# Contiguous filter features, modulation rows broadcast from DRAM, and a router product in column groups

## The chip, the cores and the metric

The kernel runs on one core of a Trainium2 chip. The metric is the device time of one execution in microseconds. TensorE (PE in the profile) multiplies a stationary operand, which it loads first (PEld), with a moving operand that streams past; VectorE (DVE), ScalarE (ACT) and GpSimd (POOL) work elementwise; SyncE (SP) issues most of the DMA transfers, in order.

## The reference

A two-layer diffusion backbone over 1024 tokens of width 1024, all in fp32. Layer 0 mixes tokens with a gated recurrence (RG-LRU) and with Hyena, which convolves with long filters that a small network of sine layers makes from positions. Layer 1 mixes with a Conformer convolution. Behind each mixer stands a mixture of 16 experts, in which every expert takes the 128 tokens that score highest for it. All parts are modulated by six vectors of width 1024 per layer, made from a conditioning vector c.

```python
# the modulation, per layer
sh1, sc1, g1, sh2, sc2, g2 = split(silu(c) @ w_mod[l] + b_mod[l], 6)
# Hyena's filters: n = 1024 positions, 2 orders, 2 directions, 512 channels
hid = sin(freq[0] * (z @ filt_w1 + filt_b1))
hid = sin(freq[1] * (hid @ filt_w2 + filt_b2))        # 1024 x 64
filt = (hid @ filt_w3 + filt_b3) * window
kf = rfft(two_sided(filt))
# behind each mixer
xl = xl + g1 * mixer(modulate(rmsnorm(xl, n1), sh1, sc1))
h = modulate(rmsnorm(xl, n2), sh2, sc2)
probs = softmax(h @ router[l], over tokens)
gates, idx = top_k(probs, 128)                         # per expert
xl = xl + g2 * scatter_add(idx, experts(h[idx]) * gates)
```

## The kernel before

**Stages.** In the order of the profiled span: constants, the filter network and the first modulation vectors (0 to 22 us); Hyena's filters, with the norm and transposes of x between them (22 to 158); the input projection and the RG-LRU (to 300); Hyena itself (to about 573), with the rest of the modulation between; the opening of w_out (to 603); the posts of layer 0, which are output projection, residual, norm and router, tile by tile of 128 tokens, with the sorting for the top tokens (to 737); the experts of layer 0 (743 to 1322); the conformer (to 1550); the posts of layer 1 (to about 1700) and its experts (1723 to 2300); the final norm.

**Order of work.** A tile framework puts the instructions of every engine in order and sets the semaphores. It does so by itself, except at the end of `even_mixer`, where PE, DVE and ACT follow the written order. SP's queue is in order: a transfer that waits holds up all behind it. `wr` is a ring of four buffers of 128 x 2048 through which the w_mod, w_in, kd and w_out loads and some results pass.

**Big products.** They run as three matmuls (L153 to L155, `mm3` or its like) on a high and a low part, which `split` makes with a ScalarE cast and a VectorE subtraction. For w_out these are `wide_hi` (L958, the cast oh) and `wide_lo` (L963, the subtraction ol).

**Filters.** `sin_layer` writes the hidden features to h2, 65 rows (the 65th is one, for the bias) by 1024 positions. `signal` in `filters` (L377 to L391) makes the filters of 128 channels, one order and both directions: for each residue a of the position modulo 8 a matmul (L387) with h2[:, a::8] as stationary operand, 65 x 128 with a step of 8 elements, and 128 columns of ws moving; L388 multiplies four of them by the window, to sd. There are 8 such jobs of 16 matmuls. The products with the Fourier matrix G follow (L410 q0, L414 and L415 qa, L419 and L420 qb), then a chain of small VectorE steps (L432 to L448), and the write to kd in DRAM (L449) from a `wr` buffer. `ada` work (L225) and the transposes of x (L302) are put between by the generator `other`.

**Modulation.** `ada_mm` (L225) multiplies silu(c) with w_mod, in four column groups, and `ada_end` turns the result into columns: mod (128 x 48, a column per 128 features) and gg, the norm weight times one plus the scale. In Hyena's stage `fill` does a part of this between other steps. `bcast` (L258 to L266) makes a 128 x 1024 tile with a row's value in all partitions out of eight such columns: eight fp32 matmuls (L264) of a column broadcast to 128 x 128 with the identity, and two ScalarE copies (L266). It is called four times a layer: g1b and G2b (`mix_cast`), sh2b (`even_mixer` and `mix_more`), g2b (the experts, behind the index copy `ixq`).

**Posts and router.** `post` (L1000 to L1032) makes tile t of x1; `post_t` transposes x1 (L1039) and copies it to hT (L1041); `post_r` (L1044 to L1050) multiplies hT, eight blocks of 128 x 128, stationary, with the 16 columns of R2 = router * gg for each, moving, and adds the rest on VectorE (L1050). They are called for the tile before, between the matmuls of the present one. From tile 3 on VectorE sorts (L879, L882) beside that.

**End of Hyena in layer 0.** `hy_inv` and its like end with VectorE steps L607 to L614 and L558 to L575, then products with IG (L625), zt (L633), and the split of y and z. In the written order after it stand the openings `wide_hi` and `wide_lo` of w_out, the broadcasts, and the split. The gate ge (ACT L716, DVE L717) is written to ycd (SP L718).

Of the kernel before, what the change touches and what calls it, by code (L numbers as in the profile page):

```python
# [9 lines left out]
F32 = mybir.dt.float32  # L10
# [135 lines left out]
class Builder:  # L146
# [22 lines left out]
    def consts(self):  # L169
# [5 lines left out]
        nc.gpsimd.memset(self.idn, 0.0)  # L175
        nc.gpsimd.affine_select(self.idn, self.idn, pattern=[[-1, 128]], compare_op=OP.not_equal,
                                fill=1.0, base=0, channel_multiplier=1)
        it = T.tile([128, 128], I32, name="it")
        nc.gpsimd.iota(it, pattern=[[1, 128]], base=0, channel_multiplier=0)
        self.iota = P.tile([128, 128], F32, name="iota")  # L180
# [54 lines left out]
    def ada_end(self, l, s, q):  # L235
        nc = self.nc
        r = self.wr.tile([128, 512], F32, name="w", tag="w")
        nc.scalar.copy(r, q)
        t = self.ps.tile([128, 512], F32, name="t", tag="n")
        for b in range(4):  # L240
            nc.tensor.transpose(t[:, b * 128:(b + 1) * 128], r[:, b * 128:(b + 1) * 128], self.idn)
        tv = t.rearrange("p (b j x) -> p j b x", b=4, j=4, x=32)
        nc.vector.tensor_tensor(self.mod[l][:, s * 16:(s + 1) * 16].rearrange("p (j b) -> p j b", j=4),
                                tv[:, :, :, 0], self.v(f"bm{l}", s * 16, 16).rearrange("p (j b) -> p j b", j=4),
                                op=OP.add)
        if l == 0 and s == 0:
            nc.vector.tensor_tensor(self.modc.rearrange("p (j b) -> p j b", j=4),
                                    tv[:, :, :, 1], self.v("bm0", 0, 16).rearrange("p (j b) -> p j b", j=4),
                                    op=OP.add)
            nc.vector.scalar_tensor_tensor(self.ggc, self.modc[:, 8:16], 1.0, self.v("n1g0"), op0=OP.add, op1=OP.mult)  # L250
        if s == 0:
            nc.vector.scalar_tensor_tensor(self.gg[l][0], self.mod[l][:, 8:16], 1.0, self.v(f"n1g{l}"),
                                           op0=OP.add, op1=OP.mult)
        if s == 2:
            nc.vector.scalar_tensor_tensor(self.gg[l][1], self.mod[l][:, 32:40], 1.0, self.v(f"n2g{l}"),
                                           op0=OP.add, op1=OP.mult)

    def bcast(self, dst, col):  # L258
        nc = self.nc
        for h in range(2):  # L260
            q = self.ps.tile([128, 512], F32, name="q", tag="n")
            for c in range(4):
                k = h * 4 + c
                nc.tensor.matmul(q[:, c * 128:(c + 1) * 128], col[:, k:k + 1].to_broadcast([128, 128]), self.idn,  # L264
                                 start=True, stop=True)
            nc.scalar.copy(dst[:, h * 512:(h + 1) * 512], q)  # L266

    def rstd(self, pool, ss, n=1):
        nc = self.nc
# [43 lines left out]
    def sin_layer(self, pool, q, m, fcol, bcol, dst):  # L313
        nc = self.nc
        x = pool.tile([128, 512], F32, name="sx", tag="sx", bufs=2)[:m]
        k = pool.tile([128, 512], F32, name="sk", tag="sk", bufs=2)[:m]
        nc.scalar.activation(x, q, AF.Identity, bias=bcol, scale=fcol)
        nc.vector.tensor_scalar(k, x, 1.0 / (2.0 * math.pi), MAGIC, op0=OP.mult, op1=OP.add)
        nc.vector.tensor_scalar(k, k, -MAGIC, None, op0=OP.add)
        nc.vector.scalar_tensor_tensor(x, k, -TWO_PI_HI, x, op0=OP.mult, op1=OP.add)  # L320
        nc.vector.scalar_tensor_tensor(x, k, -TWO_PI_LO, x, op0=OP.mult, op1=OP.add)
        nc.vector.tensor_scalar(x, x, PI_IN, -PI_IN, op0=OP.min, op1=OP.max)
        nc.scalar.activation(dst, x, AF.Sin, bias=0.0, scale=1.0)

    def filt_mlp(self, p, f):
# [9 lines left out]
        nc.sync.dma_start(w3, A["fw3"].rearrange("k (g c) -> k g c", g=4))  # L335
        self.G = p.tile([128, 8, 256], F32, name="G")
        self.Gn = p.tile([128, 3, 256], F32, name="Gn")
        self.h2 = h2 = p.tile([65, D], F32, name="h2")
        self.ws = ws = p.tile([65, 2, 2, 512], F32, name="ws")
        self.fbias = p.tile([1, 2, 512], F32, name="fbias")  # L340
        nc.gpsimd.memset(h2[64:65, :], 1.0)
        fq, b1, b2 = self.v("fq"), self.v("fb1"), self.v("fb2")
        fb = f.tile([128, 2], F32, name="fb")
        V.tensor_tensor(fb[:, 0:1], fq[:, 0:1], b1, op=OP.mult)
# [5 lines left out]
        for n in range(2):  # L350
            q = self.ps.tile([128, 512], F32, name="q", tag="n")
            nc.tensor.matmul(q[:64], w2[:, n], h1, start=True, stop=True)
            self.sin_layer(f, q[:64], 64, fq[:64, 1:2], fb[:64, 1:2], h2[:64, n * 512:(n + 1) * 512])
        w3v = w3.rearrange("k (o d) c -> k o d c", o=2)
        for o in range(2):
            V.tensor_tensor(ws[:, o, 0], w3v[:, o, 0], w3v[:, o, 1], op=OP.add)
# [14 lines left out]
    def filters(self, fk, other):  # L371
# [5 lines left out]
        def signal(qd, o):  # L377
# [5 lines left out]
            for i in range(2):  # L383
                for a in range(0, 8, 4):
                    q = self.ps.tile([128, 4, 128], F32, name="q", tag="n")
                    for j in range(4):
                        nc.tensor.matmul(q[:, j], h2[:, a + j:D:8], ws[:, o, i, cs], start=True, stop=True)  # L387
                    V.tensor_tensor(sd[:, i, a:a + 4], q, win[:, a:a + 4], op=OP.mult)  # L388
            V.tensor_tensor(sd[:1, 0, 0], sd[:1, 0, 0], sd[:1, 1, 0], op=OP.add)
            V.scalar_tensor_tensor(sd[:1, 0, 0], sd[:1, 0, 0], 0.5, self.fbias[:, o, cs], op0=OP.mult, op1=OP.add)  # L390
# [254 lines left out]
    def even_mixer(self, st, so):  # L645
# [7 lines left out]
        with ExitStack() as s1, ExitStack() as sl:  # L653
# [164 lines left out]
            with tc.tile_pool(name="pq0", bufs=1, reuse_waits="tile") as pq, \  # L818
# [5 lines left out]
                    self.wide_hi(po, ws[q])  # L824
                    self.wide_lo(po, ws[q], q)
                self.mix_cast(0)
                self.bcast(self.sh2b, self.mod[0][:, 24:32])
                self.wide_hi(po, ws[2])
                z = drain()
                self.split(th, tl, y)  # L830
# [85 lines left out]
    def mix_open(self, l, st, st2):  # L916
# [12 lines left out]
        self.W = [pm.tile([128, 128], F32, name=f"W{i}") for i in range(2)]  # L929
        self.S = [pm.tile([128, 128], F32, name=f"S{i}") for i in range(2)]  # L930
        self.nc.vector.memset(self.W[1][64:96], 0.0)
        self.R2 = pm.tile([128, 8, NE], F32, name="R2")
        self.cb = pm.tile([128, NE], F32, name="cb")

    def mix_cast(self, l):
        self.bcast(self.g1b, self.mod[l][:, 16:24])
        self.bcast(self.G2b, self.gg[l][1])

    def mix_more(self, l):
        if l:  # L940
            self.bcast(self.sh2b, self.mod[l][:, 24:32])
        self.nc.vector.tensor_tensor(self.R2, self.router, self.gg[l][1][:, :, None].to_broadcast([128, 8, NE]), op=OP.mult)
        q = self.ps.tile([128, 512], F32, name="q", tag="n")
        for c in range(8):
            self.nc.tensor.matmul(q[:, :NE], self.mod[l][:, 24 + c:25 + c].to_broadcast([128, 128]), self.router[:, c],
# [88 lines left out]
    def post_t(self, x, hT, b):  # L1034
        nc = self.nc
        q = self.ps.tile([128, 512], F32, name="q", tag="n")
        for j in range(4):
            c = b * 4 + j
            nc.tensor.transpose(q[:, j * 128:(j + 1) * 128], x[:, c * 128:(c + 1) * 128], self.idn)  # L1039
        h = self.pm.tile([128, 4, 128], F32, name="hT", tag="hT", bufs=3)  # L1040
        nc.scalar.copy(h, q)  # L1041
        hT.append(h)

    def post_r(self, t, hT, r):  # L1044
        nc = self.nc
        V = nc.vector
        q = self.ps.tile([128, 512], F32, name="q", tag="n")
        for c in range(8):
            nc.tensor.matmul(q[:, :NE], hT[c // 4][:, c % 4], self.R2[:, c, :], start=c == 0, stop=c == 7)  # L1049
        V.scalar_tensor_tensor(self.lg[:, t], q[:, :NE], r, self.cb, op0=OP.mult, op1=OP.add)  # L1050
        if t == 3:
            self.todo += [lambda: self.soft(0), self.group0]
# [125 lines left out]
    def experts(self, l):  # L1178
        nc, tc, A = self.nc, self.tc, self.A
        V = nc.vector  # L1180
        with tc.tile_pool(name=f"pe{l}", bufs=1, side="right", reuse_waits="tile") as pe:
# [83 lines left out]
            with tc.issue_after(getattr(self.last, "ins", self.last)):  # L1265
                for _ in range(4):
                    self.moe_load(nc.gpsimd)
            with tc.issue_after(self.ixq):
                self.bcast(g2b, self.mod[l][:, 40:48])
            fetch(1)  # L1270
            for b in range(2):
                transx(0, b)
# [264 lines left out]
    def build(self):  # L1537
        nc, tc, A = self.nc, self.tc, self.A
        with ExitStack() as st:
# [5 lines left out]
            self.kd = [[dr.tile([128, 8, 2, 128], F32, name=f"kd{o}{h}") for h in range(4)] for o in range(2)]  # L1545
            self.ycd = dr.tile([D, D], F32, name="ycd")
            self.hsd = dr.tile([512, D], F32, name="hsd")
            self.acc = [dr.tile([D, D], F32, name=f"acc{l}") for l in range(2)]
            self.h2d = [dr.tile([D, D], F32, name=f"h2d{l}") for l in range(2)]
            self.ud = [dr.tile([128, D], F32, name=f"ud{n}") for n in range(8)]  # L1550
# [78 lines left out]
```

## Time and profile before

| | |
|---|---|
| three runs | 2336.77, 2337.35, 2340.97 us; median 2337.35 |
| span of the profiled execution | 2336.7 us |
| granted TensorE clock, mean | 0.959 of full speed |
| PE / DVE / ACT busy | 94% / 78% / 52% |
| data moved | 611.9 MB, 262 GB/s |
| the costliest lines | L153 to L155 (big products), their casts (L158) and subtractions (L159) |

The profiled execution's own time is its span, 2336.7 us, some 0.7 under the median. Its critical chain follows, from the last instruction back, what released each step; its lines are the start, the duration and what ran, with x for the number of passes of a matmul. An fp32 matmul has two passes. A row of a group gives line, engine, operation, out<-in, partitions x elements, the count, then busy time, the mean of one, and the idle time before it with what ended it.

### The profile page before, as it was taken

The page shows a single profiled execution, that of the slowest core. Times are in us where ns is not written, and L with a number is a line of the kernel's source. Part 1 is how long each engine was busy: PE and PEld are TensorE (multiplying, and loading weights), DVE is VectorE, ACT ScalarE, POOL GpSimd, SP SyncE. Part 2 cuts the span into 40 slices and gives each one's busy share as a digit, 9 for nine tenths or more (in the row PEclk, how much of TensorE's full clock was granted, in tenths as well). Part 3 has the DMA queues.
Part 4 walks back from the last instruction along what each step waited for, and adds up shares of the span by engine and source line. Part 5 has one row for each costly group of instructions (what it writes and reads, how often), then busy time and mean ns, then how long its engine had stood idle before and what let it go on. Part 6 is the DMA issues. An engine that isn't in the chain of part 4 may idle for free.

```text
span 2336.7 us, 29325 instructions
## 1 busy us (share of the span) xinstructions
PE 2195.2 (94%) x10970; PEld 1734.1 (74%) x10970; DVE 1820.5 (78%) x2871; ACT 1203.8 (52%) x1454; POOL 126.8 (5%) x128
## 2 busy tenths in 40 slices
PE   7999999998995999999999699989869999999997
PEld 5987765776883787787787578878747777777775
DVE  4577888998586898898988642455968888988887
ACT  2537921123221777777777531134237676776775
POOL 0000000000001000000000100010010000000001
PEclk8889999999997999999999899989979999999999
DMA  6341277554657999999998634424579999999974
GB/s 232 108 145 45 81 299 279 198 201 184 207 184 278 338 377 393 375 383 385 379 391 302 180 120 117 136 73 180 186 290 371 374 369 386 369 378 379 367 283 153
DMA packets 208776, 611.91 MB, mean 262 GB/s; under 512 B 27828, under 2 KB 76534, under 8 KB 198841
## 3 DMA queue, kind: packets, MB, share of 16 engines
q1 hardware_dynamic: 197386, 568.62, 64.6%
q0 software_dynamic: 11248, 41.42, 7.2%
q8 instruction: 86, 1.41, 0.2%
q14 instruction: 56, 0.46, 0.1%
HBM read 554.43 MB, written 55.57 MB: 261 GB/s over the span
## 4 chain that ended last, share of the span: by engine, by line
PE 82%; DVE 9%; DMA 4%; ACT 2%; issue 1%; SPq 0%; POOL 0%; POOLq 0%; ACTq 0%; DVEq 0%
PE P L153 20%; PE P L155 20%; PE P L154 20%; PE P L1237 6%; PE q L387 3%; PE q L1202 2%; PE q L225 2%; PE q L586 1%; PE q L625 1%; PE q L1049 1%; DMA w<-i_w_mod 1%; DMA wx<-i_exp_w 1%; PE q L503 1%; PE q L1368 1%; PE q L302 1%
## 5 line engine op out<-in xcount | busy, mean ns | idle before, releaser
L159 DVE TENSOR_TENSOR e<-wx,e 128x1024 fp32r<-128x1024 f32 x516 | 618.9, 1221 | 92.4 <-ACT e L158 78.4
L158 ACT CAST e<-wx 128x1024 fp32r<-128x1024 f32 x516 | 540.9, 1053 | 231.6 <-PE P L155 231.0
L153 PE MATMUL P<-e,th 128*128 128x512 f32 x1384 | 562.5, 406 | 0.2 <-ACT th L158 0.2
L155 PE MATMUL P<-e,tl 128*128 128x512 f32 x1384 | 543.3, 393 | 1.6 <-DVE tl L159 1.6
L154 PE MATMUL P<-e,th 128*128 128x512 f32 x1384 | 542.7, 392 | 0.0
L154 PEld LDWEIGHTS P<-e,th 128*128 128x128 f32 x1384 | 260.6, 188 | 60.5 <-DVE e L159 4.3
L153 PEld LDWEIGHTS P<-e,th 128*128 128x128 f32 x1384 | 260.4, 188 | 60.6 <-issue 7.2
L155 PEld LDWEIGHTS P<-e,tl 128*128 128x128 f32 x1384 | 260.1, 188 | 60.4 <-DVE tl L159 2.5
L159 DVE TENSOR_TENSOR e<-w,e 128x1024 fp32r<-128x1024 f32 x176 | 211.8, 1222 | 50.9 <-ACT e L158 28.3
L153 PE MATMUL P<-hh,wh 128*128 128x512 f32 x576 | 229.3, 399 | 8.1 <-DVE y L762 4.2
L158 ACT CAST e<-w 128x1024 fp32r<-128x1024 f32 x176 | 183.8, 1050 | 95.1 <-PE P L155 75.6
L155 PE MATMUL P<-hh,wlo 128*128 128x512 f32 x576 | 228.7, 397 | 1.8 <-DVE wlo L159 1.8
L154 PE MATMUL P<-hl,wh 128*128 128x512 f32 x576 | 229.1, 398 | 0.7 <-DVE ms L271 0.7
L153 PEld LDWEIGHTS P<-hh,wh 128*128 128x128 f32 x576 | 109.4, 190 | 42.9 <-issue 19.3
L155 PEld LDWEIGHTS P<-hh,wlo 128*128 128x128 f32 x576 | 109.4, 190 | 28.4 <-issue 4.0
L154 PEld LDWEIGHTS P<-hl,wh 128*128 128x128 f32 x576 | 109.2, 190 | 28.2 <-issue 5.2
L1301 POOL DMA_INDIRECT acc<-yo,ix x31 | 50.7, 1634 | 933.1 <-DVE yo L1300 933.1
L159 DVE TENSOR_TENSOR tl<-q,th 128x512 fp32r<-128x512 f32 x128 | 84.6, 683 | 6.6 <-ACT th L158 4.7
L158 ACT CAST wh<-w 128x1024 fp32r<-128x1024 f32 x16 | 16.7, 1049 | 136.7 <-PE P L154 124.2
L1237 PE MATMUL P<-wx,xf 128*128 128x512 f32 x176 | 79.1, 592 | 0.0
L1041 ACT COPY hT<-q 128x512 f32<-128x512 f32 x32 | 18.6, 588 | 110.4 <-PE q L1039 110.4
L158 ACT CAST th<-q 128x512 fp32r<-128x512 f32 x128 | 71.6, 585 | 1.8 <-PE q L1202 1.8
(403 smaller groups left out, 3216.5 us busy)
## 6 DMA issues: line engine op xcount, KB each, us to landing
wx<-i_exp_w SPq DMA_DIRECT2D x272, 1024.0 KB, 7.9
w<-i_exp_w SPq DMA_DIRECT2D x96, 1024.0 KB, 7.9
w<-i_w_mod SPq DMA_DIRECT2D x48, 1024.0 KB, 8.0
wst<-i_w_in SPq DMA_DIRECT2D x20, 512.0 KB, 5.1
kd<-w SPq DMA_DIRECT2D x8, 1024.0 KB, 5.2
w<-kd SPq DMA_DIRECT2D x8, 1024.0 KB, 7.0
acc<-res SPq DMA_DIRECT2D x16, 512.0 KB, 2.9
e<-i_exp_w SPq DMA_DIRECT2D x16, 512.0 KB, 5.9
```

The costliest lines, as they stand in the source:

```text
L153: t.matmul(o, lh, rh, start=start, stop=False)
L154: t.matmul(o, lh, rl, start=False, stop=False)
L155: t.matmul(o, ll, rh, start=False, stop=stop)
L158: self.nc.scalar.copy(hi, src)
L159: self.nc.vector.tensor_sub(lo, src, hi.bitcast(F32))
L225: self.nc.tensor.matmul(self.ada_q[32 * j:32 * j + 32, :], self.sp[:, kc, :], w[:, j * 512:(j + 1) * 512], start=kc == 0, stop=kc == 7, ti ...
L302: nc.tensor.transpose(q[:, t * 128:(t + 1) * 128], x[:, c * 128:(c + 1) * 128], self.idn)
L387: nc.tensor.matmul(q[:, j], h2[:, a + j:D:8], ws[:, o, i, cs], start=True, stop=True)
L503: nc.tensor.matmul(q[:, :n], W, xa[:, o:o + n], start=True, stop=True)
L1202: nc.tensor.transpose(q[:, j], src[:, c * 128:(c + 1) * 128], self.idn)
L1237: nc.tensor.matmul(P[:, ns], f[:, k], h[:, ns], start=k == 0, stop=k == 7)
L1301: self.last = nc.gpsimd.indirect_dma_start(self.acc[l][:, :], bass.IndirectOffsetOnAxis(ap=xT[e][1][:, 0:1], axis=0), yo, None, compute_op ...
```

## The change

There are three parts. First, h2 is stored as 65 x 8 x 128, by residue, so that the stationary operand of L387 is contiguous; `sin_layer` writes it in the order of positions through a view with 128 elements between neighbours. Second, for the last four of the six vectors, `ada_end` transposes the columns to rows (two matmuls), copies them to a `wr` buffer (the r that it has already), and writes them to a DRAM tensor rowd of 4 x 1024; `bcast` is then one DMA of a row to all 128 partitions. The order that g2b had behind `ixq` is gone. Third, the router: R2, padded with zeros to 32 columns for each block, is the stationary operand, each of its eight blocks in one of four column groups of 32, with the 128 tokens of hT moving. This gives four partial sums in four groups of partitions; ScalarE copies them to L4, and one more matmul, with a 128 x 16 matrix of four stacked identities, adds and transposes them. hT has two buffers instead of three.

The core of the diff:

```diff
@@ consts
+        self.stack = P.tile([128, NE], F32, name="stack")
+        nc.vector.tensor_tensor(self.stack, self.idn[:, 0:NE], self.idn[:, 32:32 + NE], op=OP.add)
+        for g in (64, 96):
+            nc.vector.tensor_tensor(self.stack, self.stack, self.idn[:, g:g + NE], op=OP.add)
@@ ada_end, bcast
-
-    def bcast(self, dst, col):
-        nc = self.nc
-        for h in range(2):
+        cols = {1: [self.mod[l][:, 16:24], self.mod[l][:, 24:32]], 2: [self.gg[l][1], self.mod[l][:, 40:48]]}
+        if s in cols:
             q = self.ps.tile([128, 512], F32, name="q", tag="n")
-            for c in range(4):
-                k = h * 4 + c
-                nc.tensor.matmul(q[:, c * 128:(c + 1) * 128], col[:, k:k + 1].to_broadcast([128, 128]), self.idn,
-                                 start=True, stop=True)
-            nc.scalar.copy(dst[:, h * 512:(h + 1) * 512], q)
+            for i, col in enumerate(cols[s]):
+                nc.tensor.transpose(q[:8, i * 128:(i + 1) * 128], col, self.idn)
+            rows = r[:8, :256].rearrange("c (i p) -> c i p", i=2)
+            nc.scalar.copy(rows, q[:8, :256].rearrange("c (i p) -> c i p", i=2))
+            nc.sync.dma_start(self.rowd[l][2 * s - 2:2 * s].rearrange("i (c p) -> c i p", p=128), rows)
+
+    def bcast(self, dst, l, i):
+        self.nc.sync.dma_start(dst, self.rowd[l][i:i + 1, :].to_broadcast([128, D]))
@@ sin_layer, filt_mlp, signal
+        if len(dst.shape) == 3:
+            x = x.rearrange("m (p a) -> m p a", a=8)
         nc.scalar.activation(dst, x, AF.Sin, bias=0.0, scale=1.0)
...
-        self.h2 = h2 = p.tile([65, D], F32, name="h2")
+        self.h2 = h2 = p.tile([65, 8, 128], F32, name="h2")
...
-                        nc.tensor.matmul(q[:, j], h2[:, a + j:D:8], ws[:, o, i, cs], start=True, stop=True)
+                        nc.tensor.matmul(q[:, j], h2[:, a + j], ws[:, o, i, cs], start=True, stop=True)
@@ mix_open, post_t, post_r
-        self.R2 = pm.tile([128, 8, NE], F32, name="R2")
+        self.R2 = pm.tile([128, 8, 32], F32, name="R2")
+        self.nc.vector.memset(self.R2, 0.0)
...
-        h = self.pm.tile([128, 4, 128], F32, name="hT", tag="hT", bufs=3)
+        h = self.pm.tile([128, 4, 128], F32, name="hT", tag="hT", bufs=2)
...
+        q4 = self.ps.tile([128, 512], F32, name="q", tag="n")
+        for c in range(8):
+            g = 32 * (c % 4)
+            nc.tensor.matmul(q4[g:g + 32, :128], self.R2[:, c], hT[c // 4][:, c % 4], start=c < 4, stop=c > 3,
+                             tile_position=(0, g))
+        L = self.pm.tile([128, 128], F32, name="L4", tag="L4", bufs=1)
+        nc.scalar.copy(L, q4[:, :128])
         q = self.ps.tile([128, 512], F32, name="q", tag="n")
-        for c in range(8):
-            nc.tensor.matmul(q[:, :NE], hT[c // 4][:, c % 4], self.R2[:, c, :], start=c == 0, stop=c == 7)
+        nc.tensor.matmul(q[:, :NE], L, self.stack, start=True, stop=True)
@@ the experts
-            with tc.issue_after(self.ixq):
-                self.bcast(g2b, self.mod[l][:, 40:48])
+            self.bcast(g2b, l, 3)
```

The calls of `bcast` become (self.g1b, l, 0), (self.sh2b, l, 1) and (self.G2b, l, 2).

The instructions around the edits move too. First VectorE at the end of layer 0's Hyena part, where the last inverse transform ends; before (line, operation, out<-in, size), with ge the gate, ol the low part of w_out and E the result that the last products need:

```order
L717 TENSOR_TENSOR ge<-ge,hsr 128x1024
L611 TENSOR_TENSOR sub<-E,w 128x1024
L612 TENSOR_TENSOR pq<-pq,sub 128x8x128
L717 TENSOR_TENSOR ge<-ge,hsr 128x1024
L613 TENSOR_TENSOR E<-pq 128x1024
L614 TENSOR_TENSOR E<-pq 128x1024
L558 TENSOR_TENSOR sub<-E 128x512
...
L575 SCALAR_TENSOR_TENSOR pq<-sub,E 128x2x128
L963 TENSOR_TENSOR ol<-w,oh 128x2048 x2
L633 TENSOR_TENSOR zt<-q,y 128x4x128 x2
```

In the changed kernel, whose line numbers are higher by 7 or 8 here:

```order
L724 TENSOR_TENSOR ge<-ge,hsr 128x1024
L618 TENSOR_TENSOR sub<-E,w 128x1024
L971 TENSOR_TENSOR ol<-w,oh 128x2048
L619 TENSOR_TENSOR pq<-pq,sub 128x8x128
L971 TENSOR_TENSOR ol<-w,oh 128x2048
L620 TENSOR_TENSOR E<-pq 128x1024
L621 TENSOR_TENSOR E<-pq 128x1024
L565 TENSOR_TENSOR sub<-E 128x512
...
L582 SCALAR_TENSOR_TENSOR pq<-sub,E 128x2x128
L640 TENSOR_TENSOR zt<-q,y 128x4x128 x2
```

The two ol of the first w_out quarters have moved from behind the chain into it, and one ge stands earlier.

Second, SP's queue at the same place, from the last load of kd to the first residual tile; before:

```order
L580 DMA w<-kd_76 128x2048
L714 DMA hsr<-hsd 128x1024
L951 DMA w<-i_w_out 128x2x1024 x3
L714 DMA hsr<-hsd 128x1024
L718 DMA ycd<-ge 128x1024
L951 DMA w<-i_w_out 128x2x1024
L718 DMA ycd<-ge 128x1024
L908 DMA yc<-ycd 128x7x128
L1567 DMA res<-i_x 128x1024
```

In the changed kernel, with the row writes (rowd) and the broadcasts (g1b, G2b, sh2b):

```order
L587 DMA w<-kd_76 128x2048
L721 DMA hsr<-hsd 128x1024
L959 DMA w<-i_w_out 128x2x1024 x2
L725 DMA ycd<-ge 128x1024
L721 DMA hsr<-hsd 128x1024
L271 DMA g1b<-rowd_79 128x1024
L271 DMA G2b<-rowd_79 128x1024
L725 DMA ycd<-ge 128x1024
L268 DMA rowd_80<-w 8x2x128
L959 DMA w<-i_w_out 128x2x1024 x2
L915 DMA yc<-ycd 128x7x128
L271 DMA sh2b<-rowd_79 128x1024
```

The third and fourth w_out quarters now stand behind a row write (here layer 1's last), which waits for ScalarE's copy.

Third, TensorE at the router product of tile 1 of layer 0, before, with the moving operand named first and the stationary one second:

```order
L1049 MATMUL q<-R_4247,hT 128x16 x8
L153 MATMUL P<-oh,zh 128x512
L154 MATMUL P<-ol,zh 128x512
L155 MATMUL P<-oh,zl 128x512
L153 MATMUL P<-oh,th 128x512
```

And in the changed kernel:

```order
L1058 MATMUL q<-hT,R_4240 32x128 x8
L153 MATMUL P<-oh,zh 128x512
L154 MATMUL P<-ol,zh 128x512
L1063 MATMUL q<-stack,L_4439 128x16
L155 MATMUL P<-oh,zl 128x512
```

Two big products stand between the column groups and the product that adds them, which has to wait for ScalarE's copy L.

More of the change, by code (lines that the diff above doesn't have):

```diff
@@ L337, in filt_mlp @@
         self.Gn = p.tile([128, 3, 256], F32, name="Gn")
-        self.h2 = h2 = p.tile([65, D], F32, name="h2")
+        self.h2 = h2 = p.tile([65, 8, 128], F32, name="h2")
         self.ws = ws = p.tile([65, 2, 2, 512], F32, name="ws")
         self.fbias = p.tile([1, 2, 512], F32, name="fbias")
-        nc.gpsimd.memset(h2[64:65, :], 1.0)
+        nc.gpsimd.memset(h2[64:65], 1.0)
         fq, b1, b2 = self.v("fq"), self.v("fb1"), self.v("fb2")
@@ L352, in filt_mlp @@
             nc.tensor.matmul(q[:64], w2[:, n], h1, start=True, stop=True)
-            self.sin_layer(f, q[:64], 64, fq[:64, 1:2], fb[:64, 1:2], h2[:64, n * 512:(n + 1) * 512])
+            self.sin_layer(f, q[:64], 64, fq[:64, 1:2], fb[:64, 1:2], h2.rearrange("k a p -> k p a")[:64, n * 64:(n + 1) * 64])
         w3v = w3.rearrange("k (o d) c -> k o d c", o=2)
@@ L826, in even_mixer @@
                 self.mix_cast(0)
-                self.bcast(self.sh2b, self.mod[0][:, 24:32])
+                self.bcast(self.sh2b, 0, 1)
                 self.wide_hi(po, ws[2])
@@ L931, in mix_open @@
         self.nc.vector.memset(self.W[1][64:96], 0.0)
-        self.R2 = pm.tile([128, 8, NE], F32, name="R2")
+        self.R2 = pm.tile([128, 8, 32], F32, name="R2")
+        self.nc.vector.memset(self.R2, 0.0)
         self.cb = pm.tile([128, NE], F32, name="cb")
     def mix_cast(self, l):
-        self.bcast(self.g1b, self.mod[l][:, 16:24])
-        self.bcast(self.G2b, self.gg[l][1])
+        self.bcast(self.g1b, l, 0)
+        self.bcast(self.G2b, l, 2)
     def mix_more(self, l):
         if l:
-            self.bcast(self.sh2b, self.mod[l][:, 24:32])
-        self.nc.vector.tensor_tensor(self.R2, self.router, self.gg[l][1][:, :, None].to_broadcast([128, 8, NE]), op=OP.mult)
+            self.bcast(self.sh2b, l, 1)
+        self.nc.vector.tensor_tensor(self.R2[:, :, 0:NE], self.router, self.gg[l][1][:, :, None].to_broadcast([128, 8, NE]), op=OP.mult)
         q = self.ps.tile([128, 512], F32, name="q", tag="n")
@@ L1547, in build @@
             self.hsd = dr.tile([512, D], F32, name="hsd")
+            self.rowd = [dr.tile([4, D], F32, name=f"rowd{l}") for l in range(2)]
             self.acc = [dr.tile([D, D], F32, name=f"acc{l}") for l in range(2)]
```

## The prediction

> **What bounds the kernel now.** I read the busy shares and the chain that ended last first, then the chain stretch by stretch, then the four stretches in which the edits lie. The page's busy row and its chain row:
>
> ```profile
> PE 2195.2 (94%) x10970; PEld 1734.1 (74%) x10970; DVE 1820.5 (78%) x2871; ACT 1203.8 (52%) x1454; POOL 126.8 (5%) x128
> ...
> PE 82%; DVE 9%; DMA 4%; ACT 2%; issue 1%; SPq 0%; POOL 0%; POOLq 0%; ACTq 0%; DVEq 0%
> ```
>
> TensorE is the bound: of the 2336.7 us span, 82% of the chain is its own. So an edit that takes passes off TensorE counts unless another engine takes over there. The profiled execution is as long as the lowest of the three runs, about 0.7 us under their median 2337.35; the sum below is made from 2336.7 and 0.6 is added at the end. About 0.2%, 4.7 us, is what a measurement of this kernel can tell from no change.
>
> The stretch with most to win is the filter stage, 22 to 158 us. Its chain (start, duration, what; x counts passes, and an fp32 matmul is two), and its load of weights against that of a neighbour:
>
> ```profile
> 122.55 7.74 PE q L387 x32
> 130.29 0.43 PE qa L414 x2
> ...
> 132.42 0.43 PE qa L415 x2
> ```
>
> ```profile
> 66.13 0.22 PE qb L419 x2
> ```
>
> ```profile
> L387 PE MATMUL q<-ws,h 65*128 65x128 f32 x256 | 63.9, 423 | 1.5 <-ACT h L323 1.5
> ...
> L420 PEld LDWEIGHTS qb<-sd,Gn 128*128 128x128 f32 x72 | 11.4, 200 | 0.0
> ```
>
> ```profile
> L387 PEld LDWEIGHTS q<-ws,h x256: 312/336/340, 21.7 to 146.6; 65*128 65x128 f32 x128
> ...
>   DVE sd L388: 18.4, 13
> ```
>
> The L387 passes come every 7.74 / 32 = 0.242 us and make a chain of their own, 256 x 0.242 = 62 us. L419 and L420, the same size of moving operand with contiguous weights, come every 0.11 us. The load is what differs: 336 ns with h2 read at a step of 8 elements, 200 ns in L420.
>
> The clock could be the reason instead. Busy time in two windows inside the block that starts at 122.55 (PE, PEld, DVE, ACT, POOL with counts, then the granted clock, DMA share and GB/s):
>
> ```profile
> 122.00:126.00 4.00, 4.00 (x21) 4.00 (x20) 2.70 (x7) 1.88 (x3) 0.00 (x0) 0.99 0.42 170
> 126.00:130.00 4.00, 4.00 (x18) 4.00 (x18) 4.00 (x12) 0.00 (x0) 0.00 (x0) 0.50 0.01 2
> ```
>
> The block has one pace through both, at clock 0.99 and at 0.50. So the load sets it, not the clock. The half clock then outlasts the block: the six pairs from 130.29 to 132.42 take 0.43 us each where a pair at full clock takes 0.22.
>
> **A, the residue layout.** Direct: 256 x (0.242 - 0.11) = 34 us less TensorE time. Following: eight blocks, each with six pairs slowed by 0.21, 10 us, if a shorter block no longer brings the half clock. That is 44 us at TensorE. What is late next:
>
> ```profile
> 21.75:158.30 136.55, 135.01 (x778) 129.05 (x779) 78.67 (x194) 50.77 (x79) 4.88 (x8) 0.79 0.36 127
> 158.30:172.00 13.70, 9.33 (x48) 7.37 (x47) 12.90 (x31) 4.91 (x8) 0.55 (x1) 0.88 0.67 221
> ```
>
> ```profile
> 99.47 3.93 DMA x<-i_x
> ```
>
> VectorE (fourth column) has 78.7 + 12.9 = 92 us of work in these 150 us, and ends the stage: from 158 us on it is busy 12.9 of 13.7 us, and TensorE 9.3. If VectorE never stood still after its first 4 us, the stage could shrink by 150 - 92 - 4 = 54 us at most, so TensorE's 44 is still the smaller saving. But the two alternate (products, then sd, then products), and one x load was already waited for, 3.9 us. At the low end only half of the direct saving survives such waits, 17. At the high end VectorE's 54 less the load's 4 is 50, for which TensorE's clock of 0.79 in the stage would have to come near 1 throughout. I take 35: all of the direct 34, half of the 10, less the load wait of 4. That is nearest to the passes' own row. Range 17 to 50.
>
> A's other side, from the chain:
>
> ```profile
> 20.98 0.64 ACT h L323
> ```
>
> The two strided writes of h2 by ScalarE (this is one) and three tiny additions for the stack tile stand on the chain before 21.75. From nothing to twice the writes' 0.64 each: +0.7, between 0 and 1.5.
>
> The Trainium skill, in "TensorE: Matmul & The Clock Gate", section "LDWEIGHTS (loading the stationary operand)", speaks against A: a load takes its columns / 1.2 in ns, and the number of columns alone counts. For 128 columns that would be an estimated 107 ns with either layout, and A would win nothing. The 336 against 200 ns of the rows above disagree; the measurement decides here.
>
> **B, rows through DRAM.** Sixteen passes for each of 8 broadcasts and their two ScalarE copies go; four pairs of transposes, four small copies, four row writes and eight 512 KB broadcast loads come. What the passes cost depends on the place.
>
> End of layer 0's Hyena part, from the timeline (start, duration, engine, line):
>
> ```profile
> 573.13 1.95 PE L264 MATMUL q<-idn,mod 128*128 128x128 f32 x16
> 573.33 1.02 ACT L716 ACTIVATE ge<-P 128x1024 f32<-128x1024 f32 x1 [9.39 <-PE P L155]
> 574.25 3.69 ACT L958 CAST oh<-w 128x2048 fp32r<-128x2048 f32 x2
> 574.77 1.22 DVE L717 TENSOR_TENSOR ge<-ge,hsr 128x1024 f32<-128x1024 f32 x1
> 575.90 1.22 DVE L613 TENSOR_TENSOR E<-pq 128x1024 f32<-128x1024 f32 x1
> 583.74 0.41 DVE L575 SCALAR_TENSOR_TENSOR pq<-sub,E 128x256 f32<-128x256 f32 x1
> 584.08 4.48 DVE L963 TENSOR_TENSOR ol<-w,oh 128x2048 fp32r<-128x2048 f32 x2
> 584.21 6.22 PE L625 MATMUL q<-IG,pq 128*128 128x128 f32 x28 [3.23 <-DVE pq L575]
> ```
>
> The three broadcasts here (from 573.13) lie beside the VectorE chain that ends at 584.15 and that TensorE waits 3.2 us for. Removing them gains nothing. But the scheduler's new order puts the two ol subtractions (4.48 us, until now behind the chain and beside L625's 6.2 us) into that chain, ahead of L613, and takes one ge (1.2) out of it. ol needs the oh cast, which needs the ge activation at 573.33: ge ends near 575.5, the next step 576.7, ol 578.9, one more step 580.1, the second ol 582.4, and the 8.25 us from L613 to the end of L575 then end at 590.6 in place of 584.15: +6.5. If the casts and the ge come earlier by what the shorter filter stage and the changed order leave, it is 4.5 - 1.2 = +3. I take +5, between 1 and 8. On SP's queue the row write stands ahead of two w_out loads and waits for its copy; the third cast comes behind the first two, which end at 577.9, so those loads have some cover.
>
> Hyena part itself: the new transposes need mod and gg from VectorE, which has a backlog. The one set that shows the most, with TensorE's transposes (chain), VectorE's reading of them, and two waits for w_mod loads that are on the chain already:
>
> ```profile
> 389.30 0.44 PE t L241 x4
> ...
> 403.40 4.95 DMA w<-i_w_mod
> ```
>
> ```profile
> L243 DVE TENSOR_TENSOR mod<-t,vec x1: 159/159/159, 403.7 to 403.7; 128x16 f32<-128x16 f32 x1
> ```
>
> ```profile
> 306.16 9.84 DMA w<-i_w_mod
> ```
>
> mod is written 14 us after the transposes. The new rows stand in TensorE's order 3, 42, 10 and 41 rows behind the L241 transposes (an L586 or L153 pass is 0.11 to 0.23 us, so 0.5 to 10 us of cover), and the row write stands on SP's queue in front of w_mod loads, with its buffer taken from the ring of four that these loads use. Each of four sets can cost from nothing to a wait like the 4.95. I take +3, range 0 to 9.
>
> Layer 1's opening, chain and ScalarE:
>
> ```profile
> 1562.11 0.43 PE q L264 x2
> ...
> 1563.81 2.85 PE q L264 x14
> 1566.66 1.69 PE q L945 x16
> ```
>
> ```profile
> 1565.44 1.19 ACT L1481 ACTIVATE sT<-q,vec 128x128 f32<-128x128 f32 x3
> ```
>
> Here sh2b's 3.28 us are on the chain. Without them TensorE is up against ScalarE's sT, which ends at 1566.6 with two copies of 0.6 gone from behind it. I take -2.5, range -3.3 to 0.
>
> g2b, both layers, and the price of a broadcast load:
>
> ```profile
> 736.98 5.28 DMA xs<-h2d,ix
> ```
>
> ```profile
> L264 PE MATMUL q<-idn,mod x16: 421/421/561, 736.3 to 739.7; 128*128 128x128 f32 x16
> ```
>
> ```profile
> b2b<-i_cf_b SPq DMA_DIRECT2D x1, 512.0 KB, 8.3
> ```
>
> g2b's passes, from 736.3 to about 740, lie beside the wait for the gather: gain 0. A broadcast load lands in about 8 us, and g1b, G2b and sh2b are first read in the posts, behind L625 and w_out's casts: 0, up to +1.
>
> **C, the router.** Two tiles before; a product in two column groups (64 passes); the busy times in the posts; a ScalarE copy of 128 columns:
>
> ```profile
> 627.03 1.69 PE q L1049 x16
> ...
> 640.97 1.69 PE q L1049 x16
> ```
>
> ```profile
> 1416.03 3.65 PE q L1368 x64
> ```
>
> ```profile
> 640.00:700.00 60.00, 59.54 (x313) 49.01 (x311) 47.91 (x197) 12.20 (x22) 3.11 (x4) 1.00 0.51 183
> ```
>
> ```profile
> L1084 ACT COPY W<-q x6: 258/258/267, 663.6 to 1698.4; 64x128 f32<-64x128 f32 x4, 128x128 f32<-128x128 f32 x2
> ```
>
> Sixteen passes cost 0.106 each. In column groups: 0.057 by L1368, so 0.9 us, or no better than 0.106, so 1.69. The stack product adds two passes, 0.2, two big products behind (0.46 us of cover against a copy of 0.26 plus two handovers). So 1.1 to 1.9 a tile, and 0.5 more if the copy is late: I take 1.3, -0.4 a tile. VectorE is busy 80% of the time from 640 on and sets the last tiles, so some ten of sixteen count: -4, less 1 for the copies in ScalarE's queue: -3, range -8 to +8 (half a microsecond a tile either way).
>
> The Trainium skill, "TensorEngine Tiling (Array Packing)", section "Key Properties", says that changing the tiling mode drains the TensorE. That would be two drains a tile, a price against this edit that no row here shows by itself.
>
> **Sum.** 2336.7 - 35 + 0.7 + 5 + 3 - 2.5 - 3 = 2304.9, plus 0.6: 2305.5 us.
>
> **The rivals.**
> - Next limit: the filter stage alternates between TensorE and VectorE so tightly, or waits for kd writes and x loads on SP, that only 17 us survive, with B and C as summed: 2323.5. For: the load at 99.47 and the tail aren't TensorE's. Against: VectorE is busy 78.7 of 136.6 us there and has room. That is 2305.5 + 18. 0.13.
> - VectorE never stands still: the stage gives 50, and the opening costs 2 instead of 5: 2305.5 - 15 - 3 = 2287.5. For: it is busy for 58% of the stage already and has a backlog at its end. Against: the 18.4 us that sd waited for products. 0.12.
> - The layout doesn't set the pace (65 rows, or the moving side do): A gives 0, and the rest is +3.2: 2336.7 + 3.2 + 0.6 = 2340.5. Against: the 336 ns and the pace that the clock leaves alone. For: no row has contiguous weights of 65 rows. 0.04. The page named under A would have it so.
> - Slower through the ring: each of four row buffers holds one of four ring slots and SP's queue while VectorE is behind, and each then costs a wait like the 9.84 us of 306, 39 us in place of 3. Then 2305.5 + 36 = 2341.5. It decides from some 9 us a set, about twice the wait of 403. For: mod is 14 us late once. Against: three of four sets have cover or a small lag. 0.03.
>
> **Chances.** Forecast 0.68 (2296 to 2315 by itself). The range takes in the first two rivals and no more: 2287 to 2325. Faster 0.93: forecast and the first two rivals. The last two hold 0.07; both lie at the edge of what counts, and C at its best end would bring them back: slower 0.05, same 0.02.
>
> **What would show it.** A: the load of L387's successor near 200 ns, its blocks near 3.6 us, clock above 0.9 in the stage; wrong if the load stays at 336, or if TensorE's idle time in the stage grows to tens of us. B: L575's end some 5 us later behind L613; no new waits for w_mod above 5 us; a shorter stretch at 1562. C: 1.1 to 1.5 us a tile, and the tile period from 13.95 to about 13.5 us; wrong if the stack product waits for the copy L.

## The result and the profile after

The changed kernel takes 2297.95 us (median of 4 runs, 2295.77 to 2303.67) against 2338.6 before (4 runs on the same chip): ratio 0.9827, 95% interval 0.9812 to 0.9842, 41 us less. The forecast was 2305.5, range 2287 to 2325. The span of its profiled execution is 2295.1 us, 41.6 less than the 2336.7 before, and the steps below are read from these two.

The page of the changed kernel, busy row and chain row:

```profile
PE 2123.7 (93%) x10882; PEld 1654.9 (72%) x10882; DVE 1819.8 (79%) x2876; ACT 1201.7 (52%) x1458; POOL 127.1 (6%) x128
...
PE 77%; DVE 14%; DMA 3%; issue 3%; ACT 2%; POOL 1%; SPq 0%; POOLq 0%; ACTq 0%; DVEq 0%
```

TensorE lost 71 us of busy time, the span 41.6; VectorE's share of the chain rose from 9% to 14%. L387 is L394 now. The filter stage in the chain (start, duration, what), and the load of L394:

```profile
21.04 1.08 ACT h L330
22.26 6.60 PE q L394 x32
...
37.21 3.57 PE q L394 x32
```

```profile
75.59 4.25 DMA x<-i_x
...
94.32 3.57 PE q L394 x32
...
108.01 0.69 DVE hl L159
...
128.45 0.34 DVE kT L450
128.93 0.76 PE P L153
```

```profile
L394 PEld LDWEIGHTS q<-ws,h x256: 186/192/333, 22.2 to 109.2; 65*128 65x128 f32 x128
```

The load went from 336 to 192 ns and a pass from 0.242 to 0.112 us. The last two rows show what is late next: from 108 us on the chain is VectorE's, step after step, until it goes over to the input projection at 128.93; before, it did so at 167.24. The stretch from 22 to that point, and from 108 on (us, then PE, PEld, DVE, ACT, POOL busy, granted clock, DMA share, GB/s):

```profile
22.26:128.93 106.67, 98.67 (x806) 93.21 (x807) 85.40 (x215) 53.07 (x83) 4.89 (x8) 0.95 0.49 169
108.00:129.00 21.00, 15.88 (x133) 14.92 (x132) 20.92 (x55) 6.29 (x10) 0.00 (x0) 0.99 0.53 152
```

The clock is 0.95 where it was 0.79, and VectorE works 20.9 of the last 21 us.

The end of layer 0's Hyena part on VectorE, from the timeline:

```profile
531.68 1.22 DVE L724 TENSOR_TENSOR ge<-ge,hsr 128x1024 f32<-128x1024 f32 x1
532.81 1.22 DVE L618 TENSOR_TENSOR sub<-E,w 128x1024 f32<-128x1024 f32 x1
533.95 2.28 DVE L971 TENSOR_TENSOR ol<-w,oh 128x2048 fp32r<-128x2048 f32 x1
536.15 1.22 DVE L619 TENSOR_TENSOR pq<-pq,sub 128x1024 f32<-128x1024 f32 x1
537.28 2.28 DVE L971 TENSOR_TENSOR ol<-w,oh 128x2048 fp32r<-128x2048 f32 x1
539.49 1.21 DVE L620 TENSOR_TENSOR E<-pq 128x1024 f32<-128x1024 f32 x1
...
547.32 0.42 DVE L582 SCALAR_TENSOR_TENSOR pq<-sub,E 128x256 f32<-128x256 f32 x1
```

The two ol stand in the chain as forecast, 4.4 us in all.

The opening of layer 1, in the chain:

```profile
1518.00 1.77 POOL lrs L1457
...
1521.14 1.09 PE q L953 x6
1522.24 1.36 PE q L1489 x6
1523.60 1.96 PE q L953 x10
...
1525.58 0.04 DVE cb L955
...
1525.67 0.55 DVE Y L1481
...
1526.36 0.66 PE q L1489 x2
...
1531.71 0.24 PE P L153
```

sh2b's passes are gone, but L953, the product for cb, has taken their place among the transposes (L1489). cb's copy on VectorE waits for it, the next Y (L1481) stands behind that copy, and TensorE stops until Y is there. It runs at half clock (0.43 us for one big pass) until 1531.71, 13.7 us after lrs; before, the big passes ran at full clock from 1568.68, 9.7 us after lrs:

```profile
1558.96 1.77 POOL lrs L1444
...
1568.68 0.24 PE P L154
```

The router in two neighbouring tiles of each layer, from the chain:

```profile
589.27 0.57 PE q L1058 x16
590.50 0.17 PE q L1063 x2
...
602.47 0.57 PE q L1058 x16
```

```profile
1547.45 0.57 PE q L1058 x16
1561.16 0.57 PE q L1058 x16
```

Sixteen passes take 0.57 us in place of 1.69, and the period of a tile falls from 13.94 to 13.20 us in layer 0. In layer 1 it is 13.71; the rows of before for that stretch:

```profile
1587.18 1.69 PE q L1049 x16
1601.91 1.69 PE q L1049 x16
```

That was 14.73.

### The profile page after: what moved, and what is told of

It is laid out like the page before. It is cut to its first block, busy times and chain, and to the rows that moved or that the text cites. A ratio compares the mean times of both kernels' runs of the same rounds, so it can differ in the third digit from the quotient of the medians.

```text
span 2295.1 us, 29201 instructions
## 1 busy us (share of the span) xinstructions
PE 2123.7 (93%) x10882; PEld 1654.9 (72%) x10882; DVE 1819.8 (79%) x2876; ACT 1201.7 (52%) x1458; POOL 127.1 (6%) x128
## 4 chain that ended last, share of the span: by engine, by line
PE 77%; DVE 14%; DMA 3%; issue 3%; ACT 2%; POOL 1%; SPq 0%; POOLq 0%; ACTq 0%; DVEq 0%
PE P L153 20%; PE P L155 20%; PE P L154 19%; PE P L1251 6%; PE q L1216 2%; PE q L593 1%; PE q L229 1%; PE q L394 1%; PE q L510 1%; PE q L632 1%; PE q L1381 1%; PE q L307 1%; POOL rs L278 1%; DVE mm L873 0%; DMA xs<-h2d,ix 0%
## 5 line engine op out<-in xcount | busy, mean ns | idle before, releaser
L153 PEld LDWEIGHTS P<-hh,wh 128*128 128x128 f32 x576 | 108.8, 189 | 40.4 <-issue 13.2
L278 POOL TENSOR_TENSOR rs<-ms,nh 128x1 f32<-128x1 f32 x42 | 23.9, 570 | 830.1 <-issue 435.2
```

The source lines that it names most:

```text
L153: t.matmul(o, lh, rh, start=start, stop=False)
L278: nc.gpsimd.tensor_tensor(r, m, self.nh[:, :n], op=OP.pow)
```

## The experiments

Ratios are to runs of the kernel before on the same chip. Where a kernel was run once, its trace carries the verdict.

### The three parts alone

`a_only` is the kernel before with the residue layout (`sin_layer` writes it as in the change):

```diff
-        self.h2 = h2 = p.tile([65, D], F32, name="h2")
+        self.h2 = h2 = p.tile([65, 8, 128], F32, name="h2")
-    nc.tensor.matmul(q[:, j], h2[:, a + j:D:8], ws[:, o, i, cs], start=True, stop=True)
+    nc.tensor.matmul(q[:, j], h2[:, a + j], ws[:, o, i, cs], start=True, stop=True)
```

> The kernel before with h2 stored by residue and nothing else. If the load of the strided weights set the pace of the filter stage and VectorE is the next limit, the stage ends 37 us earlier, as it does in the changed kernel, and the rest is as before: 2301 us (2297 to 2305). If part of the 37 us came from the other two edits' new order, the stage gains less than 30 us and the time is above 2308.

2299.93 us, ratio 0.9828 (0.9812 to 0.9845). The layout alone gives 40 us, as much as the whole change.

`b_only` has the rows through DRAM alone (the new `ada_end` and `bcast` of the diff, and g2b without its wait):

```diff
-                nc.tensor.matmul(q[:, c * 128:(c + 1) * 128], col[:, k:k + 1].to_broadcast([128, 128]), self.idn, ...)
+        self.nc.sync.dma_start(dst, self.rowd[l][i:i + 1, :].to_broadcast([128, D]))
```

> The kernel before with rows through DRAM and nothing else. As the changed kernel's trace reads (Hyena 2.4 us earlier, opening of layer 0 3.3 us later, opening of layer 1 1 us later), the time is 2340 us, within 3 us of before. As I forecast (3 and 5 us lost, 2.5 gained) it is 2344. If TensorE's passes of the broadcasts were on the path at more places than I saw, it is below 2334.

2344.36 us, ratio 1.0016 (1.0006 to 1.0026): slower by 1.4 to 6 us. The edit that takes 128 passes off TensorE loses.

`c_only` has the router in column groups alone (the new `post_r`, R2, stack and two hT buffers):

```diff
+            nc.tensor.matmul(q4[g:g + 32, :128], self.R2[:, c], hT[c // 4][:, c % 4], start=c < 4, stop=c > 3,
+                             tile_position=(0, g))
+        nc.tensor.matmul(q[:, :NE], L, self.stack, start=True, stop=True)
```

> The kernel before with the router in column groups and nothing else. If the product costs 0.57 us plus 0.4 us for the stack product instead of 1.69, on ten to fourteen tiles that TensorE sets, the time is 2331 us (2328 to 2334). As I forecast (0.4 us a tile) it is 2336. If ScalarE's copy holds TensorE up in its queue, 2339 or more.

2331.84 us, ratio 0.9967 (0.9953 to 0.9982): 8 us, 4 to 11.

The sum of the three, -40, +4 and -8, is -44; the change measured -41, within the intervals.

### What makes the load slow

Here the stationary operand of the filter products is read at a step of s elements, with h2 stored as 65 x 8/s x 128 x s:

```diff
-        self.h2 = h2 = p.tile([65, D], F32, name="h2")
+        self.h2 = h2 = p.tile([65, 2, 128, 4], F32, name="h2")
-    nc.tensor.matmul(q[:, j], h2[:, a + j:D:8], ...)
+    nc.tensor.matmul(q[:, j], h2[:, (a + j) // 4, :, (a + j) % 4], ...)
```

> The kernel before with h2 stored so that the stationary operand is read at a step of 4 elements (16 bytes) in place of 8. If what counts is that each element comes from a 16-byte line of its own, the load stays at 336 ns, the passes at 0.24 us and the time near 2338. If the cost grows with the step, the load is between 192 and 336 ns and the time between 2301 and 2338. If only a step of 8 or more hurts, 192 ns and 2301.

2334.83 us. Its load of weights, a block in the chain, and its filter stage:

```profile
L389 PEld LDWEIGHTS q<-ws,h x256: 308/329/332, 21.5 to 145.4; 65*128 65x128 f32 x128
```

```profile
37.65 7.57 PE q L389 x32
```

```profile
22.00:157.00 135.00, 133.39 (x773) 128.93 (x773) 78.27 (x192) 50.94 (x79) 4.89 (x8) 0.76 0.36 126
```

A step of 16 bytes is as slow as one of 32: 329 ns, 0.237 us a pass. With the step of 2 (in the diff 4 becomes 2 and 2 becomes 4):

> The kernel before with the stationary operand of the filter products read at a step of 2 elements (8 bytes). A step of 4 gave the same 330 ns and 0.24 us a pass as one of 8. If two elements to a 16-byte line are enough, this is 192 ns, 0.11 us a pass and 2300 us. If any step is slow, 330 ns and 2336. If the number of lines counts in proportion, about 260 ns, 0.17 us a pass and 2318.

2299.61 us, and in its trace:

```profile
L389 PEld LDWEIGHTS q<-ws,h x256: 194/196/200, 21.8 to 107.1; 65*128 65x128 f32 x128
```

```profile
32.10 3.77 PE q L389 x32
```

```profile
22.00:127.00 105.00, 98.97 (x808) 93.95 (x807) 85.91 (x215) 53.35 (x83) 4.74 (x8) 0.95 0.50 175
```

196 ns and 0.118 us a pass, almost the contiguous 192 and 0.112. So the cost sets in between 8 and 16 bytes, and from 16 to 32 it hardly grows. The rows of the two windows also settle the clock: the kernel with the slow load has 0.76 in the stage, the one with the fast load 0.95, with the same matmuls (the second window holds some 35 passes more). That the half clock follows the slow blocks was read from one block in the prediction; these two kernels show it.

The Trainium skill, "Advanced Engine Details and Errata", section "SBUF Cachelines", speaks of lines of 16 bytes and of at least two hits on a line for full speed. The trace agrees: two elements to 16 bytes run at the full pace, one doesn't. Whether the lines are the reason or any step above 8 bytes is slow, these steps don't tell apart. The rule of the Trainium skill in "TensorE: Matmul & The Clock Gate", section "LDWEIGHTS (loading the stationary operand)", by which the number of columns alone counts, doesn't hold here.

### What the row edit costs, and what it would gain

Two edits undo the changes of order that came with it. `ol_late` holds the first two ol until the last inverse transform is done:

```diff
+                    with tc.issue_after(self.fft_last):
-                    self.wide_lo(po, ws[q], q)
+                        self.wide_lo(po, ws[q], q)
```

(fft_last is the last instruction of the latest inverse transform, L582.)

> The changed kernel with the first two ol subtractions held until the last inverse transform of Hyena is done, as they stood before. If they cost the opening of layer 0 what the trace shows (4.5 us in the chain, one ge less), the last step of that chain comes 3 to 4.5 us earlier and the time is 2294 to 2295. If their 4.5 us only move behind the IG products and hold up zt there, less than 1.5 us are won: 2297.

2295.42 us, ratio 0.9802 (0.9785 to 0.9819). Its VectorE:

```profile
543.14 0.42 DVE L582 SCALAR_TENSOR_TENSOR pq<-sub,E 128x256 f32<-128x256 f32 x1
543.48 4.49 DVE L973 TENSOR_TENSOR ol<-w,oh 128x2048 fp32r<-128x2048 f32 x2
547.88 1.13 DVE L641 TENSOR_TENSOR zt<-q,y 128x512 f32<-128x512 f32 x1
549.65 1.12 DVE L641 TENSOR_TENSOR zt<-q,y 128x512 f32<-128x512 f32 x1 [0.65 <-PE q L633]
```

The chain ends at 543.14 in place of 547.32, and the second zt at 549.65 in place of 553.19: 3.5 us. In the times, 0.9802 against 0.9827 points the same way, but the intervals overlap.

`cb_early` issues the product for cb in layer 1 when the posts are set up:

```diff
                     self.mix_open(1, s2, s3)
+                    self.mix_more(1)
...
                         def later():
-                            self.mix_more(1)
```

> The changed kernel with the product for cb and its copy issued when the posts of layer 1 are set up, ahead of the statistics of the layer norm. If cb's copy in front of the second Y on VectorE, and the half clock that follows the stop, made up for sh2b's passes, the first tile of layer 1 comes 3 to 4 us earlier and the time is 2294.5. If the ScalarE chain of sT sets that opening anyway, less than 1 us: 2297.5.

2294.87 us, ratio 0.9796 (0.9781 to 0.9811). In its chain the opening reads:

```profile
1525.46 2.63 POOL lrs L1457
...
1530.85 1.16 ACT sT L1494 x3
1532.01 0.52 ACT sTh L158
1532.57 0.50 PE P L153
1533.07 0.23 PE P L154
```

ScalarE's sT is the next limit, as the prediction had it for this place, and the big passes run at full clock from 1533.07, 7.6 us after lrs. That is 6 us better than in the changed kernel and 2 better than before. Over the whole stretch from lrs to the second gather less is left of it: 151.4 us against 154.3 in the changed kernel.

`b_mended` is the kernel before with the rows through DRAM and these two edits, the diffs of `b_only`, `ol_late` and `cb_early`, nothing else:

> The kernel before with rows through DRAM alone, and with the two order edits: ol held until the last inverse transform, and cb's product of layer 1 early. By itself the row edit was at 1.0016. If its loss was the order that came with it (3.5 us at the opening of layer 0, 4.6 at that of layer 1), it now gains: ratio 0.998, 2334 us. If the loss lies in the transfers and the waits for them, it stays at 1.001.

2336.63 us, ratio 0.9982 (0.9973 to 0.9991). The same row edit that lost 1.6 parts in a thousand now gains 1.8. The transfers are the same in both, so the loss was the order that came with them. (The kernel before with the early cb alone was not run; `a_c_cb`, below, has it without the row edit, beside A and C, and gains nothing there.)

### The wait for L

`l_late` splits `post_r` and puts the stack product into the next half of the tile:

```diff
                 if n == 0 and k == 6 and yp is not None:
-                    self.post_r(t - 1, yp[2], yp[1])
+                    L = self.post_r(t - 1, yp[2], yp[1])
+                if n == 1 and k == 0 and yp is not None:
+                    self.post_r2(t - 1, L, yp[1])
```

> The changed kernel with the stack product moved four big product groups back, from two products behind the column groups to the first group of the next half. TensorE waits 0.2 to 0.35 us for the copy L a tile. If that wait is on the path, 16 x 0.25 less the tiles that VectorE sets: 2 to 3 us, 2295.5. If VectorE's sorting takes it up, or lg comes too late for it, no change or slower: 2298 or more.

2296.48 us, ratio 0.9819 (0.9801 to 0.9837), not to be told from the changed kernel. TensorE's wait for L, in the changed kernel and here:

```profile
  ACT L L1061: 5.0, 17
```

```profile
  ACT L L1063: 3.1, 7
```

The wait was 5.0 us in all and shrank to 3.1. The tiles show nothing of that either: a period of 13.16 us in place of 13.20 in layer 0, 13.76 in place of 13.71 in layer 1.

### Better than both

`all_three` is the changed kernel with `ol_late`, `cb_early` and `l_late` together:

> The three edits of the other kernels of this call together. If they lie in different places and add up: 4 + 3.5 + 2.5 = 10 us, 2288. If each only uncovers the next limit: 2295 or more.

2289.37 us, ratio 0.9778 (0.9765 to 0.9792): the fastest of all, 11 us below the changed kernel by the ratios, whose intervals lie apart, as the sum had it. `a_plus_c` is the changed kernel without the row edit, the diffs of `a_only` and `c_only` together:

> The changed kernel without rows through DRAM: the residue layout and the column groups alone, with the broadcasts by matmuls as before. If the three edits add up (40 and 8 us gained, 4.5 lost), this is 48 us below before, ratio 0.9795, and 4 to 7 us faster than the changed kernel. If the row edit only loses with the old router or the old filter stage beside it, this is no faster than the changed kernel: ratio 0.983.

2294.45 us, ratio 0.9813 (0.98 to 0.9826). That is not clear of the changed kernel's 0.9827. The sum of the single parts, 0.9795, is just outside the interval, but is itself known to some 0.002 only; whether A and C lose 4 us to each other stays open. `all_three` (0.9765 to 0.9792) is clear of it: with its order mended, the row edit is worth having beside the other two. Of the edits in `all_three`, `l_late`'s is in neither `a_plus_c` nor the next kernel; by itself it could not be told from nothing. `a_c_cb` adds sh2b's broadcast and cb's product early (the diff of `cb_early`; the broadcast is in `mix_more`):

> The same, with sh2b's broadcast and cb's product of layer 1 issued when the posts are set up, ahead of the layer norm's statistics. If the opening of layer 1 is held by these 32 passes at half clock, another 5 us: ratio 0.977, the fastest of all. If the ScalarE chain of sT or the load of router comes next there, 1 us or less: ratio 0.979.

2295.39 us, ratio 0.9814 (0.9801 to 0.9828): no gain. The stretch that the edit touches, from lrs to the second gather, takes 151.5 us against 152.3 in `a_plus_c`, so what it wins there is under 1 us: the second of the two cases. The filter stage alone differs by more from kernel to kernel of the same code there (the w_mod wait behind it starts 37.2 us earlier than before in this one and 40.0 in `a_plus_c`).

## Why the prediction was right, point by point

Each term is the difference of two shifts, that of the event which ends the stretch and that of the one which begins it, between the profiles of before and after; the lines named are those of before, and a gather is a load of xs (`xs<-h2d,ix`). One profile of each kernel carries these shifts, and the profiles differ by themselves: in the nine kernels with the fast load the w_mod wait behind the filter stage starts between 264.7 and 272.1 us, and from the second gather to the end the fourteen profiles take 620.0 to 622.8 us. Terms of 2 or 3 us rest on more than this table only where other runs are named below.

| term | forecast | measured | how |
|---|---|---|---|
| start: strided writes | +0.7 | +0.5 | first filter block at 22.26 for 21.75 |
| A: filter stage | -35 | -37.9 | w_mod wait behind it starts at 268.76 for 306.16, less the +0.5 |
| Hyena | +3 | -2.2 | last L589 copy at 519.96 for 559.53 |
| opening of layer 0 | +5 | +2.3 (+3.2 at its middle) | second zt at 553.19 for 590.47; L575 at 547.32 for 583.74 |
| posts, both layers (C) | -3 | -3.1 and -4.6 | to the gather: 696.56 for 736.98 (shift -40.4), and 1672.25 for 1716.69 (-44.4) |
| opening of layer 1 | -2.5 | +1.2 | lrs at 1518.00 for 1558.96 (-41.0), first y of the posts at 1535.65 for 1575.44 (-39.8) |
| the rest | 0 | -0.5 and +2.8 | experts of layer 0 and conformer; from the second gather to the end |
| sum | -31.8 | -41.6 | |

**A was right in mechanism and near in size.** The prediction took all of the direct saving, half of what the half clock cost, and 4 us off for a load wait. The direct part is 256 x (0.242 - 0.112) = 33 us, less 3 for the first block, which still ran at half clock (6.60 us against 3.57). Of the half clock nearly all went (0.79 to 0.95), not half. For the 4 us there was no ground: the x load was waited for before too, 3.93 us, and waits 4.25 now. That makes 33 - 3 + 10, some 40 us, where 37.9 were measured; the difference is within what the profiles differ by. The first rival, that tight alternation leaves only 17 us, is refuted by `a_only`. The second has a grain of truth: VectorE sets the last 21 us. Over the whole stretch it works 85 of 107 us.

The rival that the layout doesn't set the pace fell with the row of L394: the same 65 rows, 192 ns.

**Hyena cost nothing, where +3 was forecast.** The step "each of four sets can cost from nothing to a wait like the 4.95" counted the waits that come and not those that go. The waits come: before the new transposes (L265) TensorE stands still for mod and gg of VectorE,

```profile
  DVE gg L259: 5.2, 3
  DVE mod L247: 3.1, 2
```

though how much of that it would have waited anyway no run shows. But the waits for w_mod at 403 and 523 us are gone from the chain; the second of before, and the one that remains after, ahead of Hyena:

```profile
523.15 5.90 DMA w<-i_w_mod
```

```profile
268.76 10.04 DMA w<-i_w_mod
```

That the loads came earlier because SP's queue was ordered anew is what the order suggests; no run tried it. The other kernels show both sides. From the L586 passes at 355.54 (318.40 after) to their last block, 200.3 us before, all seven kernels with the row edit take 197.7 to 199.0, and the others 200.2 to 201.5. From the w_mod wait to that point, 49.4 before, the changed kernel's profile has 49.6, but the six others with the row edit 50.5 to 51.9. So the -2.2 of the table is not shown as a gain: over the whole stretch these six come to between -1.5 and +0.4.

**The opening of layer 0** was right step by step: both ol in the chain, one ge out of it, the end of it late. It was 3.2 and not 5, as the lower of its two workings had it (4.5 - 1.2), and L625 gave back 0.9 of it (5.36 us in place of 6.22). `ol_late` takes 3.5 away. The other kernels agree: from the last L586 block to the second zt it is 36.9 to 37.9 us in the four that have the row edit without `ol_late`'s, 32.7 to 33.4 in the three that have both, 33.6 to 34.7 in those without the row edit.

**The opening of layer 1 failed** at "Without them TensorE is up against ScalarE's sT". The prediction followed the passes that go and did not ask which instruction fills their place: L953, on another engine's queue in front of Y. `cb_early` shows that sT would indeed have been next. Among the kernels with the new router, lrs to the second gather takes 152.3 us in the two with the old broadcasts and the old place of cb, 153.9 to 154.7 in the three with the row edit and cb in its old place, and 150.7 and 151.4 in the two with the row edit and cb early.

**C was undersized.** The step "0.057 by L1368, so 0.9 us, or no better" was taken from two column groups; four take 0.57 us, 0.036 a pass. A tile gained 0.74 us in layer 0 and 1.0 in layer 1, not 0.4; 3.1 and 4.6 us are four or five such tiles in each layer, as assumed. The sign set against it, that the stack product waits for L, did come (5.0 us over 17 waits, 0.3 each), and was too small to matter.

**The slow rival,** four row buffers that each cost a wait like 9.84 us, is refuted by the chain, which shows no such wait behind 278.8 us. But its sign was that of the edit: the row edit alone is slower, through order, not through the ring.

**What was luck.** The row edit was forecast at 3 + 5 - 2.5 = +5.5 us in all, and `b_only` measured +4 (1.4 to 6). That is near, but its parts were not: Hyena cost nothing instead of 3, and the opening of layer 1 lost where it should have gained 2.5. These two misses cancel. What did not cancel, A (-40 by `a_only` for -34) and C (-8 by `c_only` for -3), is why the change won more than the 31.8 us of the sum.

## What to carry to other kernels

When the load of a stationary operand takes longer than that of a neighbour of the same size, look at the step between its elements: at 4 bytes an element, a step of 2 cost nothing here and a step of 4 as much as one of 8. An edit that takes work off an engine also moves all that a scheduler orders around it; read in the new order what stands where the removed work stood, and what is queued behind it, since that was more than all of the row edit's loss here. Price an operation by the nearest row, but ask in which direction the row differs: two column groups bounded four only from one side.

## What the runs showed of the hardware that was not expected

- Column groups: sixteen passes of 128 columns in 0.57 us in four groups of 32, 0.036 us each; 0.057 in two groups of 64 (64 passes in 3.65 us); 0.11 without groups (L394). That reads as if the groups work beside each other, but no run tried other sizes.
- A transpose by TensorE is a single pass and less sensitive to the step: in the kernel before, the transposes of to_tok read a step of 8 elements, and their load takes 191 ns against 142 for a contiguous transpose (medians):

```profile
L642 PEld LDWEIGHTS q<-idn,y x32: 185/191/207, 307.1 to 504.2; 128*128 128x128 f32 x32
```

```profile
L302 PEld LDWEIGHTS q<-idn,x x144: 138/142/275, 62.4 to 1361.8; 128*128 128x128 f32 x144
```

The load is 50 ns longer there, against 140 in the filter products, and eight of them still follow each other at 0.109 us (0.87 us for eight at 503.75). So a step of 8 isn't slow everywhere: here the load stayed below the 200 ns at which L420 too runs at full pace. Why the transposes' loads suffer less no run here shows.
- A write by ScalarE with 128 elements between neighbours took 1.08 us in place of 0.64 for 64 x 512 elements, most of the start's +0.5.
